# A scheduler's estimate of times in a two-layer hybrid attention kernel: other transfer and operation times, and a port that VectorE and GpSimd share

## The chip, the cores and the metric

The kernel runs on one core of a Trainium2 chip. The metric is device time in microseconds (us) of one execution; lower is better.

## What is computed

The reference takes 1024 tokens of width 1024, puts 16 meta tokens ahead of them, and runs two layers. Each layer normalises, projects to 3588 columns, runs three mixers side by side, gates each with a SiLU, projects back and adds to the residual:

```python
for l in range(DEPTH):                       # 2
    hn = rmsnorm(h, norm_g[l])
    proj = jnp.einsum('bld,de->ble', hn, w_in[l])
    fq, fk, fv, fz, fg, dq, dk, dv, dz, pu, pz = jnp.split(proj, IN_OFFSETS, axis=-1)
    a_out = forgetting_attention(...) * jax.nn.silu(fz)      # 4 heads, causal, with a decay
    ...
    # 4 heads; each is softmax(q0 k0) - lam * softmax(q1 k1), with a distance bias
    b_out = differential_attention(...)
    b_out = rmsnorm(b_out, subln_g[l], SUBLN_EPS) * (1.0 - lambda_init)
    b_out = b_out.reshape(B, Lp, DIFF_W) * jax.nn.silu(dz)
    c_out = pooling_mixer(pu, w_pool[l], pool_scale[l]) * jax.nn.silu(pz)
    mix = jnp.concatenate([a_out, b_out, c_out], axis=-1)
    h = h + jnp.einsum('ble,ed->bld', mix, w_out[l])
y = rmsnorm(h[:, N_META:N_META + S], final_g)
```

All arithmetic is fp32 in effect: each matrix operand is split into two fp32r parts, and TensorE runs three products.

## The kernel before

The normalised input of a layer lies in SBUF (HT). The work of a layer is six "units", one after the other: two with two forgetting heads each, four with one differential head each. A unit projects V, Q and K, and runs its attention as tasks of 256 queries (`jp` 0 to 3). While one unit's attention runs, the projections of the next fill TensorE, and those of the pooling mixer fill it beside the last unit. At the end of the layer the eight mixed blocks go through the output projection.

A differential task makes these instructions. TensorE writes scores into a `psS` bank (three of them). VectorE adds the bias and takes the row minimum (the custom operation `p<-psS,dist` with its reader `mx`), ScalarE takes the exponential, VectorE makes `rd` (a reciprocal), and for the second softmax `n<-rd,nlam` and then `p<-p,n,p`, which combines the two. TensorE transposes `p` into `psT`, ScalarE and VectorE split it into two parts (`pp`), and TensorE multiplies by V into the one `psO` bank; the meta keys go the same way through the copy `m`, a transpose and `ptm`. Then comes the head's normalisation: `sq`, its parts `s` (VectorE a cast, GpSimd the rest), a product with ones, a row `v`, and three small transfers on the queue of SyncE: `rs<-v` turns the row into a column, GpSimd raises it to the power -0.5, `r_d<-rs` writes it to DRAM, and `vr<-r_d` reads it back onto all 128 partitions. VectorE multiplies the task's result by it: `sz<-sz,gs,vr`, which is called the scaling here. There are 32 scalings, 16 in a layer.

GpSimd also subtracts the parts of the weights (`ws<-wr,ws`), of the queries (`q<-rq,q`), and makes the window sums of the pooling mixer (`wa`, `wb`).

Every engine runs its instructions in the order in which they stand in its queue. This order is not the order of the code. `Order` records each instruction with its engine, its operands and an estimated duration (`note`, `cost`), and after the last one `simulate` runs a list schedule over all engines: it takes the instruction that can start first by the estimate (`free`, the end of what its engine runs; `ready`, the end of what it reads, plus `HOP`; `slots`, the time at which a buffer comes free; `way`, the longest way to the end, breaks ties). `tell` fixes the order that comes out, for TensorE, ScalarE, VectorE, GpSimd and the transfers. TensorE's instructions come from six lines (`ordr.line`), each of which keeps its own order; the estimate decides how they are merged. What work stands in which line is set earlier, by the `Clock` and the `Planner`, which the change does not touch.

Of the kernel before, what the change touches and what calls it, by code (L numbers as in the profile page):

```python
# [12 lines left out]
ALU = mybir.AluOpType  # L13
# [36 lines left out]
class Clock:  # L50

    HOP = {"act": 100, "dve": 100, "pool": 150, "dma": 1900}

# [103 lines left out]
class Order:  # L159
# [1 line left out]

    HOP = {"pe": 170, "act": 100, "dve": 100, "pool": 150, "dma": 0}

    def __init__(self):
        self.ops, self.writes, self.reads, self.rings, self.place = [], {}, {}, {}, {}
# [30 lines left out]
                at = [a + s * i for a in at for i in range(n)]  # L198
        return p0, p0 + np_, [(a, a + size) for a in at]

    def add(self, eng, ins, outs, inps, dur, tail=0):
        k, before, names = len(self.ops), set(), set()
        for aps, own, others in ((inps, self.reads, (self.writes,)), (outs, self.writes, (self.writes, self.reads))):
            for ap in aps:
                name = ap.tensor.name
                names.add(name)
                p0, p1, at = self.parts(ap)
                for lo, hi in at:
                    for other in others:
                        old = other.get(name, ())  # L210
                        before.update(e[4] for e in old if e[2] < hi and lo < e[3] and e[0] < p1 and p0 < e[1])
                        if own is self.writes and old:
                            other[name] = [e for e in old if e[0] < p0 or e[1] > p1 or e[2] < lo or e[3] > hi]
                    own.setdefault(name, []).append((p0, p1, lo, hi, k))
        before.discard(k)
        self.ops.append(dict(
            k=k, eng=eng, ins=ins, dur=dur, end=dur + tail + self.HOP[eng], before=sorted(before), stream=self.stream,
            tiles=[n for n in names if n in self.place]))

    def note(self, eng, op, ins, out, inps, extra, kw):  # L220
        dma = "dma" in op
        self.add(eng, ins, [out] + extra, inps, 350 if dma else self.cost(eng, op, out, inps, kw))
        self.ops[-1].update(dma=dma, size=4 * out.free_size() * out.partition_size() if dma else 0)

    @staticmethod
    def cost(eng, op, out, ins, kw):
        n = out.free_size()
        if eng == "act":
            pointers = sum(hasattr(kw.get(k), "tensor") for k in ("bias", "scale"))
            return 150 + 0.88 * n + 95 * pointers + (187 if kw.get("accum_out") is not None else 0)  # L230
        if eng == "dve":
            inner = sum(a.space != bass.MemoryType.PSUM and a.free_size() >= n > 1 for a in ins)
            if op == "memset":
                return 60 + 0.3 * n
            if op == "tensor_tensor_reduce":
                return 230 + 1.05 * n
            if inner == 1 and ins[0].space != bass.MemoryType.PSUM and op in ("tensor_copy", "tensor_scalar"):
                return 190 + 0.6 * n
            return 150 + (1.55 if inner > 1 else 1.05) * n
        if kw.get("op") == ALU.pow:  # L240
            return 400 + 160 * n
        return 180 + {"tensor_tensor": 2.33, "scalar_tensor_tensor": 1.5}.get(op, 3.8) * n

    def prepare(self):
        ops = self.ops
# [30 lines left out]
    def simulate(self):  # L276
        ops = self.ops
        self.prepare()
        left = [len(o["before"]) for o in ops]
        ready = [0.0] * len(ops)  # L280
        start, done = [None] * len(ops), [None] * len(ops)
        engines = ("pe", "act", "dve", "pool", "dma")
# [10 lines left out]
        for o in reversed(ops):  # L293
            if o["eng"] == "pe":
                lines.setdefault(o["stream"], []).append(o["k"])
        pe_prev = (0.0, 0.0)

        def offer(k):
            o = ops[k]
# [24 lines left out]
        while n_done < len(ops):  # L324
            best = None
            for e in engines:
                if e == "pe":
                    c = None
                    for line in lines.values():
                        if not line or left[line[-1]] or (s := slots(line[-1])) is None:  # L330
                            continue
                        load = max(pe_prev[0], pe_prev[1], ready[line[-1]], s)
                        d = (load, 0.0, line[-1], max(free["pe"], load + 105), e)
                        if c is None or d < c:
                            c = d
                    if c is None:
                        continue
                else:
                    c = None
                    for k in waiting[e]:  # L340
                        s = slots(k)
                        if s is None:
                            continue
                        t = max(free[e], ready[k], s)
                        d = (t, -ops[k]["way"], k, t, e)
                        if c is None or d < c:
                            c = d
                    if c is None:
                        continue
                if best is None or c < best:  # L350
                    best = c
            assert best is not None, "no instruction can go on"
            _, _, k, t, e = best
            o = ops[k]
            start[k] = t
            for n in o["tiles"]:
                if self.first[n] == k:
                    tag, i = self.place[n]
                    begun[tag] = i + 1
                    if i >= self.rings[tag][0]:  # L360
                        g = min(gone[tag])
                        gone[tag].remove(g)
                        taken[n] = g[1]
                    else:
                        taken[n] = None
            free[e] = t + o["dur"]
            end = t + o["end"]
            if e == "pe":
                lines[o["stream"]].pop()
                pe_prev = (t, best[0] + 105)  # L370
            else:
                waiting[e].remove(k)
            if e == "dma":
                bus = max(bus, t + 350) + o["size"] / 300.0
                end = max(t + 350 + 1900, bus + 1500)
            done[k] = end
            order[e].append(k)
            n_done += 1
            for n in o["tiles"]:
                uses[n] -= 1  # L380
                lastuse[n] = max(lastuse.get(n, 0.0), end)
                if not uses[n]:
                    gone[self.place[n][0]].append((lastuse[n], n))
            for a in o["after"]:
                left[a] -= 1
                if e != "pe" or ops[a]["eng"] != "pe":
                    ready[a] = max(ready[a], end)
                if not left[a] and ops[a]["eng"] != "pe":
                    offer(a)
# [17 lines left out]
def hymba(  # L407
# [93 lines left out]
    def transpose(o, src, ident):  # L501
        r = nc.tensor.transpose(o, src, ident)  # L502
        clk.pe(o, [src], 0.84 * o.free_size())
        ordr.add("pe", r.ins, [o], [src, ident], 0.447 * o.free_size() + 4.5)

    xs, tail = [], None

# [1028 lines left out]
```

## Time and profile before

| | |
|---|---|
| median of 3 runs | 1269.38 us (1265.15 to 1269.6) |
| the profiled execution, its own time | 1262.05 us |
| its span, from the first to the last instruction | 1260.3 us |

The span and its own time differ by 1.75 us, which lie around the first and the last instruction. In the profile PE is TensorE, DVE is VectorE, ACT is ScalarE, POOL is GpSimd and SP is SyncE; line L148 is the helper through which all operations but those of TensorE are issued, so that groups are told apart by the names of their tiles. A tile's number is left out there. A busy time of PE contains matrix products that overlap, so idle time, and what ended it, tells more than the share.

### The profile page before, as it was taken

What the parts mean: (1) busy time and instruction counts of PE and PEld (TensorE: products, weight loads), DVE (VectorE), ACT (ScalarE), POOL (GpSimd) and SP (SyncE); (2) the same over time, 40 slices, a digit from 0 to 9 for tenths busy, and PEclk for the clock granted to TensorE, in tenths of its full rate; (3) what the DMA queues carried; (4) which work ended last, traced back from release to release, by engine and by line L of the source; (5) the groups of instructions that cost most, each with busy time, mean ns of one, the idle gap of its engine ahead of it and who ended that gap; (6) DMA issues with size and microseconds to landing.
All of it is one profiled execution on the core that took longest, in us unless ns stands there. A gap on an engine that the chain in (4) does not pass through costs nothing.

```text
span 1260.3 us, 21117 instructions
## 1 busy us (share of the span) xinstructions
PE 1202.6 (95%) x7644; PEld 1140.3 (90%) x7644; DVE 831.3 (66%) x2203; ACT 628.8 (50%) x1454; POOL 503.1 (40%) x584
## 2 busy tenths in 40 slices
PE   5999999999998889899999999999999999989997
PEld 4999999999998889878889999999999999989886
DVE  6556868886866848863245568688758687678422
ACT  6555655564554534453235556565545555446222
POOL 6334234345351625464313353241543525254432
PEclk9999999999999989999999999999999999999999
DMA  7121110122222232462110211111212231315431
GB/s 237 26 69 35 51 51 19 51 35 35 55 35 46 50 89 49 111 207 97 67 51 24 63 35 60 43 26 43 35 40 54 38 59 31 95 33 158 142 111 50
DMA packets 101736, 82.12 MB, mean 65 GB/s; under 512 B 19272, under 2 KB 91208, under 8 KB 101632
## 3 DMA queue, kind: packets, MB, share of 16 engines
q1 hardware_dynamic: 101488, 80.52, 24.3%
q8 instruction: 60, 0.98, 0.3%
q14 instruction: 44, 0.36, 0.1%
q10 hardware_dynamic: 144, 0.26, 0.1%
HBM read 66.92 MB, written 13.80 MB: 64 GB/s over the span
## 4 chain that ended last, share of the span: by engine, by line
PE 72%; DVE 10%; DMA 9%; POOL 3%; issue 3%; ACT 1%; SPq 0%; POOLq 0%; DVEq 0%; ACTq 0%
PE psP L496 47%; PE psS L496 13%; PE psT L502 6%; PE psO L496 6%; DMA vr<-r_d 4%; DVE p L148 4%; DMA r_d<-rs 3%; POOL q L148 1%; DVE sz L148 1%; DVE q L148 1%; POOL rs L148 1%; PE psS L502 1%; DMA x<-in_x_dram 1%; DVE pp L148 1%; DVE n L148 1%
## 5 line engine op out<-in xcount | busy, mean ns | idle before, releaser
L496 PE MATMUL psP<-HT,ws 128*128 128x346 f32 (+5 forms) x4032 | 714.8, 326 | 3.2 <-DVE Y L148 2.2
L496 PEld LDWEIGHTS psP<-HT,ws 128*128 128x128 f32 x4032 | 644.3, 190 | 5.4 <-DVE Y L148 2.6
L148 POOL TENSOR_TENSOR ws<-wr,ws 128x512 fp32r<-128x512 f32 x112 | 152.6, 1364 | 229.4 <-ACT ws L148 171.8
L148 POOL TENSOR_TENSOR q<-rq,q 64x256 fp32r<-64x256 f32 (+1 forms) x192 | 149.8, 780 | 128.8 <-DVE q L148 94.9
L148 ACT ACTIVATE p<-p,mx 128x144 f32<-128x144 f32 (+3 forms) x192 | 150.8, 786 | 76.8 <-DVE mx L148 74.2
L496 PE MATMUL psS<-K,q 128*128 128x392 f32 (+9 forms) x696 | 145.9, 330 | 9.4 <-DVE mx L148 9.4
L496 PE MATMUL psO<-pp,VV 128*128 128x256 f32 (+1 forms) x800 | 123.4, 284 | 2.1 <-DVE pp L148 2.1
L496 PEld LDWEIGHTS psS<-K,q 128*128 128x128 f32 (+1 forms) x696 | 108.6, 189 | 12.5 <-DVE mx L148 10.9
L496 PE MATMUL psP<-HT,ms 128*128 128x512 f32 (+1 forms) x504 | 115.4, 385 | 2.3 <-ACT HT L148 1.6
L148 DVE TENSOR_TENSOR pp<-psT,pp 128x512 fp32r<-128x512 f32 (+1 forms) x160 | 98.3, 632 | 23.6 <-ACT pp L148 22.0
L496 PEld LDWEIGHTS psO<-pp,VV 128*128 128x128 f32 x800 | 111.4, 191 | 2.7 <-DVE pp L148 2.6
L148 ACT ACTIVATE pp<-psT 128x512 fp32r<-128x512 f32 (+1 forms) x160 | 84.6, 551 | 58.2 <-PE psT L502 53.7
L496 PEld LDWEIGHTS psP<-HT,ms 128*128 128x128 f32 x504 | 90.6, 188 | 22.8 <-ACT HT L148 2.1
L502 PE MATMUL psT<-identf,p 128*128 128x128 f32 x576 | 88.9, 274 | 7.4 <-DVE p L148 6.7
L148 ACT ACTIVATE ws<-wr 128x512 fp32r<-128x512 f32 x112 | 70.3, 629 | 49.4 <-PE psP L496 24.5
L502 PEld LDWEIGHTS psT<-identf,p 128*128 128x128 f32 x576 | 69.0, 141 | 11.3 <-DVE p L148 8.8
L148 DVE TENSOR_SCALAR p<-p,rd 128x144 f32<-128x144 f32 (+7 forms) x128 | 77.2, 604 | 1.5
L148 DVE CUSTOM_DVE_ANT_0 p<-psS,dist 128x272 f32<-128x272 f32 (+7 forms) x128 | 62.1, 492 | 21.6 <-PE psS L496 15.8
L496 PE MATMUL psS<-HT,ms 128*128 128x512 f32 (+2 forms) x320 | 75.4, 394 | 0.0
L496 PEld LDWEIGHTS psS<-HT,ms 128*128 128x128 f32 (+2 forms) x320 | 57.6, 180 | 16.7
L148 ACT ACTIVATE K<-psP 64x346 fp32r<-64x346 f32 (+1 forms) x72 | 32.6, 453 | 74.4 <-DVE K L148 50.2
L148 POOL TENSOR_TENSOR ms<-mr,ms 128x128 fp32r<-128x128 f32 (+2 forms) x39 | 33.4, 862 | 81.9 <-ACT ms L148 81.8
(132 smaller groups left out, 1452.7 us busy)
## 6 DMA issues: line engine op xcount, KB each, us to landing
wr<-in_w_in_dram SPq DMA_DIRECT2D x112, 256.0 KB
wo<-in_w_out_dram SPq DMA_DIRECT2D x14, 512.0 KB
mr<-mix_d SPq DMA_DIRECT2D x14, 320.0 KB
cb<-c_d SPq DMA_DIRECT2D x8, 520.0 KB
x<-in_x_dram SPq DMA_DIRECT2D x8, 512.0 KB
res<-in_x_dram SPq DMA_DIRECT2D x8, 512.0 KB
h_d<-res SPq DMA_DIRECT2D x8, 512.0 KB
res<-h_d SPq DMA_DIRECT2D x8, 512.0 KB
```

Of the source, the lines that this page charges most:

```text
L148: r = f(*args, **kw)
L496: r = nc.tensor.matmul(o, w, m, start=start, stop=stop)
L502: r = nc.tensor.transpose(o, src, ident)
```

## The change

The estimate is changed in five ways, and nothing else is.

- `HOP`, the time from the end of an instruction to the start of one that waits for it, falls from 100 or 150 to 38 ns for ScalarE, VectorE and GpSimd, and rises from 170 to 200 ns for TensorE.
- A transfer was taken to land the later of 2250 ns after its issue and 1500 ns after its bytes had passed a bus of 300 bytes/ns. It now lands 1900 ns after its issue, plus its bytes at 330 bytes/ns (with the transfers queued on one bus), plus 1600 ns if it reads one row onto all partitions, or 1100 ns if its rows are shorter than 8 elements.
- VectorE's and GpSimd's operations have a flag, `port`: true for all of GpSimd's, and for those of VectorE that read SBUF alone (some copies and reductions excepted). An operation with the flag does not start before the last flagged one of the other engine has ended.
- The formulas of `cost` have other numbers; the two-input operations of VectorE in SBUF, which were taken 1.55 ns per element, are now 1.04 ns.
- TensorE's separate model of the weight load is gone; a transpose is 109 ns and no longer 62.

```diff
-    HOP = {"pe": 170, "act": 100, "dve": 100, "pool": 150, "dma": 0}
+    HOP = {"pe": 200, "act": 38, "dve": 38, "pool": 38, "dma": 0}
...
     def note(self, eng, op, ins, out, inps, extra, kw):
-        dma = "dma" in op
-        self.add(eng, ins, [out] + extra, inps, 350 if dma else self.cost(eng, op, out, inps, kw))
-        self.ops[-1].update(dma=dma, size=4 * out.free_size() * out.partition_size() if dma else 0)
+        if "dma" in op:
+            size = 4 * out.free_size() * out.partition_size()
+            more = 1600 if inps[0].ap[0][0] == 0 else 1100 if out.ap[-1][1] < 8 else 0
+            self.add("dma", ins, [out], inps, 350)
+            self.ops[-1].update(size=size, extra=more, end=2000 + more + size / 330.0)
+            return
+        dur, port = self.cost(eng, op, out, inps, extra, kw)
+        self.add(eng, ins, [out] + extra, inps, dur, port)
 
     @staticmethod
-    def cost(eng, op, out, ins, kw):
+    def cost(eng, op, out, ins, extra, kw):
+
         n = out.free_size()
+        sbuf = all(a.space != bass.MemoryType.PSUM for a in ins)
+        pointers = sum(hasattr(kw.get(k), "tensor") for k in ("bias", "scale", "scalar"))
         if eng == "act":
-            pointers = sum(hasattr(kw.get(k), "tensor") for k in ("bias", "scale"))
-            return 150 + 0.88 * n + 95 * pointers + (187 if kw.get("accum_out") is not None else 0)
-        if eng == "dve":
-            inner = sum(a.space != bass.MemoryType.PSUM and a.free_size() >= n > 1 for a in ins)
-            if op == "memset":
-                return 60 + 0.3 * n
-            if op == "tensor_tensor_reduce":
-                return 230 + 1.05 * n
-            if inner == 1 and ins[0].space != bass.MemoryType.PSUM and op in ("tensor_copy", "tensor_scalar"):
-                return 190 + 0.6 * n
-            return 150 + (1.55 if inner > 1 else 1.05) * n
-        if kw.get("op") == ALU.pow:
-            return 400 + 160 * n
-        return 180 + {"tensor_tensor": 2.33, "scalar_tensor_tensor": 1.5}.get(op, 3.8) * n
+            return 165 + 35 * sbuf + 0.835 * n + 80 * pointers + 95 * len(extra), False
+        if eng == "pool":
+            if kw.get("op") == ALU.pow:
+                return 400 + 160 * n, True
+            return 180 + {"tensor_tensor": 2.33, "scalar_tensor_tensor": 1.5}.get(op, 3.8) * n, True
+        if op == "memset":
+            return 60 + 0.3 * n, False
+        if op == "tensor_tensor_reduce":
+            return 158 + 1.05 * n + 63 * pointers, False
+        if op == "reciprocal":
+            return 157, False
+        if not sbuf or op == "tensor_tensor_scan":
+            return 150 + 1.05 * n, False
+        if op == "tensor_copy" or op == "tensor_scalar":
+            if len(ins[0].ap) > len(out.ap) or any(d[0] == 0 for d in ins[0].ap):
+                return 146 + 1.04 * n, False
+            return (146 if op == "tensor_copy" else 213) + 0.523 * n, True
+        return (150 if op == "tensor_tensor" else 220) + 1.04 * n, True
...
-        pe_prev = (0.0, 0.0)
+        port = dict.fromkeys(engines, 0.0)
...
-                        load = max(pe_prev[0], pe_prev[1], ready[line[-1]], s)
-                        d = (load, 0.0, line[-1], max(free["pe"], load + 105), e)
+                        t = max(free["pe"], ready[line[-1]] + 20, s + 20)
+                        d = (t, 0.0, line[-1], t, e)
...
+                        if ops[k]["port"]:
+                            t = max(t, port["dve" if e == "pool" else "pool"])
...
+            if o["port"]:
+                port[e] = free[e]
...
-                bus = max(bus, t + 350) + o["size"] / 300.0
-                end = max(t + 350 + 1900, bus + 1500)
+                bus = max(bus, t + 900) + o["size"] / 330.0
+                end = bus + 1000 + o["extra"]
...
-        ordr.add("pe", r.ins, [o], [src, ident], 0.447 * o.free_size() + 4.5)
+        ordr.add("pe", r.ins, [o], [src, ident], max(109, 0.447 * o.free_size() + 4.5))
```

The orders that come out hold the same instructions. Three places show how they differ. The names in the rows carry tile numbers; ISA is the custom operation with its reader.

The first is TensorE's queue in a differential unit of layer 0, at the scores of its second task (`jp` 1). `psT_5034` and `psT_5041` take the transposes of the first task, `psS_5056` and `psS_5060` are the two halves of a row of scores, and each needs a free `psS` bank. Before:

```order
753 L496 MATMUL psP_4928<-HT,ws_4664 128x346 x6
754 L496 MATMUL psP_5021<-HT,ws_4659 128x346 x12
755 L502 MATMUL psT_5034<-identf,p_4908 128x128
756 L496 MATMUL psS_5056<-K_1029_4655,q_4628 128x264 x2
757 L496 MATMUL psS_5060<-K_1029_4655,q_4628 128x264 x2
758 L496 MATMUL psP_5021<-HT,ws_4664 128x346 x3
759 L502 MATMUL psT_5034<-identf,p_4950 128x128 x2
```

And with the change:

```order
753 L511 MATMUL psP_5021<-HT,ws_4659 128x346 x12
754 L517 MATMUL psT_5034<-identf,p_4908 128x128
755 L517 MATMUL psT_5034<-identf,p_4950 128x128 x2
756 L517 MATMUL psT_5041<-identf,m_1120_5042 96x16
757 L517 MATMUL psT_5041<-identf,m_1121_5045 96x128
758 L517 MATMUL psT_5041<-identf,m_1122_5048 96x128
759 L511 MATMUL psS_5056<-K_1029_4655,q_4628 128x264 x2
760 L511 MATMUL psS_5060<-K_1029_4655,q_4628 128x264 x2
761 L511 MATMUL psP_5021<-HT,ws_4664 128x346 x12
```

The transposes of the first task now stand ahead of the scores. In VectorE's queue at the same place the scaling (`sz_3873<-sz_3873,gs_3913,vr_4935`) stood ahead of `rd_4975`, and now stands 18 instructions later, behind the bias operations of these scores and the split of the transposes. The next unit has the same two differences.

The second place is VectorE's queue in the third differential unit of layer 1, with the scaling of `vr_13186`. Before:

```order
1966 L148 COPY m_2867_13274<-p_13159 128x96
1967 L148 SCALAR_TENSOR_TENSOR sz_12155<-sz_12155,gs_12195,vr_13186 128x256
1968 L148 ISA p_13218,mx_13219<-psS_13220,dist 128x400
1969 L148 ISA mx_13219 128x1
1970 L148 ISA p_13248,mx_13249<-psS_13250,dist 128x264
1971 L148 ISA mx_13249 128x1
1972 L148 TENSOR_TENSOR pp_13267<-psT_13263,pp_13267 128x384
```

And with the change:

```order
1969 L148 COPY m_2867_13274<-p_13159 128x96
1970 L148 ISA p_13218,mx_13219<-psS_13220,dist 128x400
1971 L148 ISA mx_13219 128x1
1972 L148 ISA p_13248,mx_13249<-psS_13250,dist 128x264
1973 L148 ISA mx_13249 128x1
1974 L148 TENSOR_TENSOR pp_13267<-psT_13263,pp_13267 128x384
1975 L148 SCALAR_TENSOR_TENSOR sz_13092<-th_13243,psP_13179 128x346
1976 L148 TENSOR_TENSOR ptm_13277<-psT_13270,ptm_13277 32x256
1977 L148 SCALAR_TENSOR_TENSOR sz_12155<-sz_12155,gs_12195,vr_13186 128x256
1978 L148 ISA p_13248,mx_13249<-psS_13254,dist,mx_13249 128x264
```

The scaling let seven instructions pass, and none of the other rows shown moved. Of the 32 scalings 26 are passed by 1 to 32 instructions in this way, and six by none; one of the six is the scaling of `vr_10775`, the first of layer 1.

The third place is TensorE's queue in the second differential unit of layer 1, at the transposes of the last task (`jp` 3). `p_11815` is the output of `p<-p,n,p`. Before:

```order
1799 L496 MATMUL psP_11984<-HT,ws_11716 128x348 x6
1800 L502 MATMUL psT_12003<-identf,p_11726 128x128
1801 L496 MATMUL psP_11984<-HT,ws_11716 128x348 x6
1802 L502 MATMUL psT_12003<-identf,p_11815 128x128
1803 L502 MATMUL psT_12003<-identf,p_11726 128x128
```

And with the change:

```order
1804 L511 MATMUL psP_11984<-HT,ws_11716 128x348 x6
1805 L517 MATMUL psT_12003<-identf,p_11726 128x128
1806 L517 MATMUL psT_12003<-identf,p_11815 128x128
1807 L517 MATMUL psT_12003<-identf,p_11726 128x128
1808 L517 MATMUL psT_12003<-identf,p_11815 128x128
```

Six matrix products no longer stand between the first transpose and the one that needs `p_11815`. On VectorE the scaling and one cast of queries, which stood ahead of `p_11815<-p_11889`, now stand behind it.

## Rows read from the trace of the kernel before

**Rows 1.** The page's first part: span, then busy time, share, instructions of TensorE.

```profile
span 1260.3 us, 21117 instructions
PE 1202.6 (95%) x7644; PEld 1140.3 (90%) x7644; DVE 831.3 (66%) x2203; ACT 628.8 (50%) x1454; POOL 503.1 (40%) x584
```

**Rows 2.** Windows: stretch, length, busy time of each engine, granted clock, DMA share, GB/s.

```profile
core 0: us, PE busy (x) PEld busy (x) DVE busy (x) ACT busy (x) POOL busy (x), PEclk, DMA share, GB/s
31.50:283.50 252.00, 250.54 (x1734) 246.04 (x1733) 179.07 (x540) 144.04 (x337) 92.11 (x100) 1.00 0.16 42
283.50:535.50 252.00, 234.65 (x1532) 227.90 (x1531) 182.84 (x518) 122.76 (x287) 107.31 (x108) 0.97 0.27 59
661.50:882.00 220.50, 219.98 (x1526) 217.03 (x1525) 152.74 (x439) 126.05 (x289) 78.77 (x87) 1.00 0.15 42
882.00:1134.00 252.00, 237.41 (x1557) 232.59 (x1556) 184.98 (x501) 128.07 (x289) 109.13 (x114) 0.97 0.25 48
```

**Rows 3.** VectorE's largest wait: total, times, longest us.

```profile
DVE sz L148 <- DMA vr<-r_d: 56.1, 18, 6.7
```

**Rows 4.** Timeline of one transfer chain, layer 0: start, us, engine, instruction, idle before.

```profile
454.96 0.48 SPq L148 DMA_DIRECT2D rs<-v  x1
...
457.14 0.69 POOL L148 TENSOR_TENSOR rs<-rs,nhalf 128x2 f32<-128x2 f32 x1 [1.33 <-DMA rs<-v]
...
457.86 0.34 SPq L148 DMA_DIRECT2D r_d<-rs  x1
...
460.70 0.34 SPq L148 DMA_DIRECT2D vr<-r_d  x1
...
464.55 0.48 DVE L148 SCALAR_TENSOR_TENSOR sz<-sz,gs,vr 128x256 f32<-128x256 f32 x1 [4.78 <-DMA vr<-r_d]
...
465.18 0.57 DVE L148 CUSTOM_DVE_ANT_0 p<-psS,dist 128x400 f32<-128x400 f32 x1
...
465.82 0.81 PE L496 MATMUL psS<-K,q 128*128 128x264 f32 x2 [3.58 <-DVE mx L148]
```

**Rows 5.** Timeline, TensorE alone: other waits behind a scaling that waited.

```profile
304.53 0.71 PE L496 MATMUL psP<-HT,ws 128*128 128x346 f32 x3 [1.00 <-DVE K L148]
...
387.21 0.81 PE L496 MATMUL psS<-K,q 128*128 128x264 f32 x2 [3.25 <-DVE mx L148]
...
528.39 0.90 PE L496 MATMUL psP<-HT,ws 128*128 128x348 f32 x4 [2.20 <-DVE Y L148]
...
897.67 0.50 PE L496 MATMUL psO<-pp,VV 128*128 128x256 f32 x2 [2.07 <-DVE pp L148]
...
927.79 0.39 PE L496 MATMUL psT<-s,onesr 128*128 128x256 f32 x1 [1.55 <-DVE s L148]
...
1086.29 1.11 PE L496 MATMUL psS<-K,q 128*128 128x264 f32 x4 [2.14 <-DVE mx L148]
...
1113.50 0.39 PE L496 MATMUL psO<-ptm,VM 96*128 96x256 f32 x1 [3.48 <-DVE ptm L148]
```

**Rows 6.** Three like products at either clock, and a window behind a wait.

```profile
141.65 0.69 PE L496 MATMUL psP<-HT,ws 128*128 128x348 f32 x3
...
387.81 1.07 PE L496 MATMUL psP<-HT,ws 128*128 128x346 f32 x3
...
383.00:390.40 7.40, 4.15 (x19) 3.48 (x18) 3.68 (x14) 1.73 (x4) 1.27 (x1) 0.77 0.38 89
```

**Rows 7.** VectorE beside GpSimd: a tile's operation (ns min/median/max), then timeline.

```profile
L148 DVE TENSOR_TENSOR n<-rd,nlam x68: 136/159/3070, 231.5 to 1149.4; 128x1 f32<-128x1 f32 x64, 16x1 f32<-16x1 f32 x4
...
430.64 1.40 DVE L148 SCALAR_TENSOR_TENSOR sz<-sz,gs,vr 128x256 f32<-128x256 f32 x1 [0.54 <-DMA vr<-r_d]
...
435.13 0.55 PE L502 MATMUL psT<-identf,p 128*128 128x128 f32 x3 [2.20 <-DVE p L148]
...
1052.14 3.07 DVE L148 TENSOR_TENSOR n<-rd,nlam 128x1 f32<-128x1 f32 x1
1052.67 2.51 POOL L148 TENSOR_TENSOR ws<-wr,ws 128x512 fp32r<-128x512 f32 x2
...
1056.87 0.33 PE L502 MATMUL psT<-identf,p 128*128 128x128 f32 x1 [2.27 <-DVE p L148]
```

More of the change, by code (lines that the diff above doesn't have):

```diff
@@ L199, in parts, with add @@
         return p0, p0 + np_, [(a, a + size) for a in at]
-    def add(self, eng, ins, outs, inps, dur, tail=0):
+    def add(self, eng, ins, outs, inps, dur, port=False):
         k, before, names = len(self.ops), set(), set()
@@ L216, in add @@
         self.ops.append(dict(
-            k=k, eng=eng, ins=ins, dur=dur, end=dur + tail + self.HOP[eng], before=sorted(before), stream=self.stream,
+            k=k, eng=eng, ins=ins, dur=dur, port=port, end=dur + self.HOP[eng], before=sorted(before), stream=self.stream,
             tiles=[n for n in names if n in self.place]))
     def note(self, eng, op, ins, out, inps, extra, kw):
-        dma = "dma" in op
-        self.add(eng, ins, [out] + extra, inps, 350 if dma else self.cost(eng, op, out, inps, kw))
@@ L367, in simulate @@
             end = t + o["end"]
+            if o["port"]:
+                port[e] = free[e]
             if e == "pe":
                 lines[o["stream"]].pop()
-                pe_prev = (t, best[0] + 105)
             else:
```

## Prediction

> **What bounds the kernel now.** I read the page first, then windows, the waits of VectorE, and timelines around TensorE's waits. TensorE is busy for 1202.6 of 1260.3 us [rows 1], so an order can win no more than its 57.7 us of idle time and what a lowered clock costs. The windows show where that idle time lies. The stretches 31.5 to 283.5 and 661.5 to 882 us hold 1.46 and 0.52 us of it; 283.5 to 535.5 and 882 to 1134 us hold 17.35 and 14.59 us, and there the granted clock is 0.97 [rows 2]. These two hold most of the differential heads of the two layers, and most of the scalings.
>
> VectorE's largest wait says why: it stands idle 56.1 us in 18 waits before scalings, for the transfer `vr<-r_d` [rows 3]. One chain shows it in full [rows 4]. The three transfers were issued at 454.96, 457.86 and 460.70 us, and the scaling began at 464.55 us. From one issue to the next step the first took 2.18 us, the second 2.84 and the third 3.85; with GpSimd's step the whole took 9.59 us. The estimate of before gives each transfer some 2.25 us, so it ends about 2 us too early, and the scaling stands that much too early in VectorE's queue. Behind it stood the bias operation that frees a `psS` bank (465.18 us), and TensorE waited 3.58 us for that bank. So the reader is to see that the wait for a transfer costs nothing by itself; what stands behind it in the queue does.
>
> **The change part by part.**
>
> *Transfers.* By the new formulas `rs<-v` and `r_d<-rs` take 3.0 us each and `vr<-r_d` 3.9 us: 0.8 us over the first duration read above, 0.2 over the second, and equal to the third within 0.1. The scalings therefore move behind the work that TensorE waits for. I went through TensorE's waits that follow a waiting scaling and asked of each whether the instruction waited for now stands ahead of the scaling:
>
> - 3.58 us [rows 4] and, at 387.21, 3.25 us [rows 5]: these are the first place shown and its twin in the next unit; 18 instructions pass the scaling, and the transposes stand ahead of the scores. Both go.
> - 1.00 us at 304.53: the two `K` operations pass it. 2.20 us at 528.39: the operation that writes `Y` passes it. 1.55 us at 927.79: the cast of `s` passes it. 2.14 us at 1086.29: the second place shown. 3.48 us at 1113.50: `ptm` passes it [rows 5].
> - 2.07 us at 897.67 stays: the scaling of `vr_10775` is passed by none.
>
> The six waits to be removed, and the seventh in the timeline of the chain, sum to 3.58 + 3.25 + 1.00 + 2.20 + 1.55 + 2.14 + 3.48 = 17.2 us. The scalings themselves have no reader soon, apart from the last of a layer, so that their delay is hidden by the next unit's attention; the last scaling of layer 0 does not move and that of layer 1 moves by one instruction. Where a scaling moves less far than its transfer is late, a stall stays. At 1086.29 seven instructions pass, five of them operations; at the 0.57 us of such a row [rows 4] that is at most 2.9 us, and the transfer may be later than that. For such remainders I give back 1.7 us.
>
> *The clock.* Behind the two longest waits the granted clock falls to the lower of its two levels, 1.2 instead of 2.4 GHz: 0.77 over 383.0 to 390.4 us, and three like products take 1.07 us instead of 0.69 [rows 6]. That is 0.38 us at least. At most it is half of the 3.4 us which a mean of 0.77 implies at the lower level, 1.7 us. TensorE was also idle in a part of these 3.4 us, so I take 1.0 us for each of the two places: 2.0 us.
>
> *The port.* `n<-rd,nlam`, an operation on one column, takes 159 ns in the middle and 3070 ns once, when GpSimd ran two weight subtractions beside it [rows 7]. The two engines shut each other out. TensorE waited 2.20 us at 435.13 and 2.27 us at 1056.87 for a `p` that was late this way. At the first the scaling itself took 1.40 us ahead of `p`; the new order takes it out from there, which I count at 1.9 us of the 2.20, the scaling with the 0.54 us that it waited. At the second, the scaling moves behind `p`, but `n` still meets GpSimd: I count 0.5 us, about the time of an undisturbed scaling [rows 4]. Together 2.4 us; bounds are 0 and 4.47 us.
>
> The Trainium skill, SBUF — State Buffer, section "Who interferes with whom", says that the pair of ports is an exclusive lock, and that the second instruction blocks until the first has finished. The trace agrees that there is a lock, but the 3.07 us are longer than one GpSimd instruction beside it. By the rule the port term would be 4.47 us, by the row 2.4.
>
> *What it can cost.* The new order trusts its estimate and takes cover away. At the third place shown, six matrix products no longer stand between the first transpose and the one that needs `p_11815`; six take 1.07 x 2 = 2.1 us at the lower clock and 0.69 x 2 = 1.4 us at the higher [rows 6]. `p` is earlier there, since the scaling and a cast no longer stand ahead of it. But where a weight subtraction comes in its way, it is late by one: two took 2.51 us, so one is 1.26 us [rows 7]. I give back one, 1.3 us; the bounds are nothing and the rival below.
>
> *Hop, durations, weight load.* They move instructions by a few tenths of a microsecond at many places, under the projections that fill TensorE in the two quiet stretches (1.98 us idle in 472.5 us [rows 2]). The old figures already left almost nothing there, so I count zero, and 2 us either way. The start and the two output projections I count at nothing as well, for their products stand in the same order but for a few transposes.
>
> **The sum.** 17.2 + 2.0 + 2.4 - 1.7 - 1.3 = 18.6 us. The profiled execution took 1262.05 us, 1.75 around its span [rows 1]: 1243.5 us. The median of the runs shown is 1269.38, 0.58% above that execution; by the same ratio the forecast is 1250.7, say **1251 us**. Its own range is 1243 to 1260.
>
> **The rivals.**
>
> - *The lock is kept exactly.* If an operation that is shut out always gets in after one instruction, as the new estimate has it, both port waits go and nothing is given back: 17.2 + 2.0 + 4.5 = 23.7 us. At the far end all idle time of the two stretches but that of the quiet ones goes, 31.9 - 2.1 + 2.0 = 31.8 us. In the profile that is 1230 to 1238 us, 1237.5 to 1245.5 us on the median. This is what the rule of the Trainium skill, SBUF — State Buffer, "Who interferes with whom", makes of it. For it: most of the `n` are near 159 ns. Against it: the 3070.
> - *The stalls move.* The scalings leave, but TensorE then waits for the next thing in the same chains, `p` from ScalarE and VectorE, so that 0 to 4 us remain of the gain: 1265 to 1270 us. For it: VectorE is busy 182.84 and 184.98 us of 252 in the two stretches [rows 2], so little slack is left where work is pressed together. Against it: it stood idle for 56.1 us for transfers alone.
> - *Slower: the cover is missed.* Each of the 32 differential tasks ends with `p<-p,n,p` and its transposes. If GpSimd's subtractions fall beside `p` in most of them, each costs 1.26 us with no product left to cover it. It takes more than 18.6 + 1.3 = 19.9 us, so 16 of the 32, to be slower than before; in 30 of them it is 1262.05 - 19.9 + 37.8 = 1280 us, 1287 on the median. For it: 2.51 us of two subtractions in a row. Against it: only the two waits in the rows look like this before, and the new estimate knows of the lock.
>
> **How the numbers follow.** The forecast has 0.60, the exact lock 0.16, the moved stalls 0.16, the slower case 0.08. A change under 0.5% (6 us) can't be told from none by this measurement. The forecast and the exact lock are faster by more than that, and so is a small part of the moved stalls: 0.78. The rest of the moved stalls is no change, 0.14; slower is 0.08. The range from 1238 to 1267 us takes in the forecast, nearly all of the exact lock and half of the moved stalls; it leaves out the slower case and some 0.1 more.
>
> **What would show it.** After the change VectorE's wait for `vr<-r_d` should fall from 56.1 to under 20 us, and TensorE's idle time in the stretches of the differential heads from 31.9 to some 14 us, with fewer falls of the granted clock. The places named should hold no wait of TensorE over 1 us, apart from the one behind `vr_10775`. The forecast is wrong if the wait for `vr<-r_d` falls and the idle time of TensorE does not, with waits for `p` or `pp` in its place; or if `n<-rd,nlam` and `p<-p,n,p` grow and TensorE waits behind them in most tasks.

## The result, and the profile after

The changed kernel takes 1239.1 us (median of 4 runs, 1238.0 to 1240.6), against 1269.5 us before (4 runs, 1265.2 to 1271.2): a ratio of 0.9767, with a 95% interval of 0.974 to 0.9793. In a second measurement it was 0.9781 (0.9747 to 0.9815). It is faster, by more than the forecast of 1251 us; the time lies inside the whole range and below the forecast's own.

The page's first part, after (answers to [rows 1]):

```profile
span 1238.8 us, 21122 instructions
PE 1199.4 (97%) x7644; PEld 1136.7 (92%) x7644; DVE 805.1 (65%) x2203; ACT 628.4 (51%) x1454; POOL 499.1 (40%) x584
```

The span is 21.5 us shorter. TensorE's idle time, span less busy time, falls from 57.7 to 39.4 us, which is 18.3 of it; its busy time falls by 3.2 us with the same 7644 instructions, which fits the fewer falls of the granted clock in the windows below. VectorE's 2203 instructions take 26.2 us less, though none was removed.

Windows of the same stretches (answer to [rows 2]; the columns are those there):

```profile
31.50:283.50 252.00, 251.16 (x1733) 245.85 (x1732) 175.42 (x537) 144.00 (x335) 90.71 (x101) 1.00 0.16 41
283.50:535.50 252.00, 244.14 (x1618) 238.44 (x1618) 183.36 (x536) 132.35 (x310) 116.09 (x118) 0.99 0.32 65
661.50:882.00 220.50, 219.66 (x1518) 215.43 (x1517) 158.35 (x454) 127.55 (x293) 81.49 (x90) 1.00 0.17 45
882.00:1134.00 252.00, 244.24 (x1624) 241.29 (x1624) 184.86 (x518) 131.36 (x295) 111.29 (x116) 0.98 0.31 59
```

The two stretches of the differential heads now hold 7.86 and 7.76 us of idle time, together 15.6, where they held 31.9. Their granted clock rose from 0.97 to 0.99 and 0.98. The quiet stretches hold 1.7 us (2.0 before).

VectorE's wait for the transfer (answers to [rows 3]: total, times, longest us):

```profile
DVE sz L148 <- DMA vr<-r_d: 9.1, 5, 5.5
```

Timeline at the place of [rows 4], after:

```profile
445.04 0.48 SPq L148 DMA_DIRECT2D rs<-v  x1
...
447.83 0.69 POOL L148 TENSOR_TENSOR rs<-rs,nhalf 128x2 f32<-128x2 f32 x1 [1.76 <-DMA rs<-v]
...
448.55 0.34 SPq L148 DMA_DIRECT2D r_d<-rs  x1
...
451.19 0.34 SPq L148 DMA_DIRECT2D vr<-r_d  x1
...
456.20 0.42 DVE L148 CUSTOM_DVE_ANT_0 p<-psS,dist 128x264 f32<-128x264 f32 x1
...
457.60 0.48 DVE L148 CUSTOM_DVE_ANT_0 p<-psS,dist,mx 128x264 f32<-128x264 f32 x1
...
458.08 0.47 DVE L148 SCALAR_TENSOR_TENSOR sz<-sz,gs,vr 128x256 f32<-128x256 f32 x1
458.11 0.66 PE L511 MATMUL psS<-K,q 128*128 128x264 f32 x4
```

The transfers are no faster: over the 32 `vr<-r_d` of this kernel the time from issue to landing is 3.8 us at least, 4.3 in the middle and 6.9 at most:

```profile
DMA to landing us min/median/max: 3.8/4.3/6.9
```

So the new 3.9 us is still under the middle one, and 9.1 us of wait are left. At the place shown the scaling now begins 6.89 us after the last issue (it was 3.85), waits for nothing, and stands behind the bias operations that free the `psS` bank; the scores go on without the 3.58 us.

TensorE's own waits, after (total, times, longest us), show what is left:

```profile
PE psS L517 <- DMA identf<-in_ident_dram: 10.1, 1, 10.1
PE psP L511 <- DVE Y L148: 6.6, 2, 3.6
PE psT L517 <- DVE p L148: 4.1, 7, 0.8
PE psS L517 <- DVE wg L148: 2.9, 1, 2.9
PE psP L511 <- ACT pu L148: 2.9, 1, 2.9
```

The waits for `mx` have shrunk away and none for `p` is over 0.8 us. Besides the start, where the first and the `wg` row lie, the three waits over 1 us are those for `Y` and `pu`, in the pooling mixer at the end of each layer; together they are 9.5 us.

### The profile page after: what moved, and what is told of

Read it like the earlier page. It is cut to its first block, busy times and chain, and to the rows that moved or that the text cites. A ratio compares the mean times of both kernels' runs of the same rounds, so it can differ in the third digit from the quotient of the medians.

```text
span 1238.8 us, 21122 instructions
## 1 busy us (share of the span) xinstructions
PE 1199.4 (97%) x7644; PEld 1136.7 (92%) x7644; DVE 805.1 (65%) x2203; ACT 628.4 (51%) x1454; POOL 499.1 (40%) x584
## 3 DMA queue, kind: packets, MB, share of 16 engines
q1 hardware_dynamic: 101488, 80.52, 26.2%
## 4 chain that ended last, share of the span: by engine, by line
PE 85%; DVE 7%; ACT 3%; DMA 2%; issue 2%; SPq 0%; POOL 0%; POOLq 0%; ACTq 0%; DVEq 0%
PE psP L511 56%; PE psS L511 14%; PE psO L511 7%; PE psT L517 7%; DVE p L148 3%; DMA wo<-in_w_out_dram 1%; ACT p L148 1%; PE psS L517 1%; DVE pp L148 1%; DMA x<-in_x_dram 1%; PE psT L511 1%; DVE HT L148 0%; SPq L148 0%; DMA m<-in_m_dram 0%; DVE Y L148 0%
## 5 line engine op out<-in xcount | busy, mean ns | idle before, releaser
L148 DVE TENSOR_SCALAR p<-p,rd 128x144 f32<-128x144 f32 (+7 forms) x128 | 74.0, 582 | 1.7
L148 DVE CUSTOM_DVE_ANT_0 p<-psS,dist 128x272 f32<-128x272 f32 (+7 forms) x128 | 61.9, 490 | 12.8 <-PE psS L511 7.0
```

The lines of the kernel that those rows point to most:

```text
L148: r = f(*args, **kw)
```

## The experiments

The first runs take the change apart into transfers (the new landing times), port (the exclusion) and numbers (`HOP`, `cost`, TensorE's model). They fill all eight combinations, so each part can be read in four pairs. The kernel before ran at a median of 1259 us on the chip of `a`, `b`, `c` and `d` and at 1266 to 1269 us in the other measurements, so kernels of different chips are compared by their ratios. The changed kernel was not run on the chip of `a` to `d`; that a ratio carries over from chip to chip is assumed, not shown.

| kernel | transfers | port | numbers | ratio to before | 95% interval | TensorE idle, us | VectorE busy, us | wait for `vr<-r_d`, us |
|---|---|---|---|---|---|---|---|---|
| before | old | no | old | 1 | | 57.7 | 831.3 | 56.1 |
| a_transfers_only | new | no | old | 0.9847 | 0.9823 to 0.9871 | 46.0 | 833.8 | 9.4 |
| d_port_only | old | yes | old | 0.9912 | 0.9889 to 0.9935 | 47.5 | 797.4 | 31.0 |
| e_numbers_only | old | no | new | 1.0245 | 1.0205 to 1.0285 | 79.9 | 833.5 | 66.3 |
| f_transfers_port | new | yes | old | 0.9823 | 0.9791 to 0.9856 | 45.3 | 788.5 | 13.4 |
| c_no_port | new | no | new | 0.9895 | 0.9872 to 0.9918 | 47.3 | 835.8 | 12.8 |
| b_old_transfers | old | yes | new | 1.0063 | 1.0042 to 1.0083 | 58.7 | 804.4 | 28.2 |
| after | new | yes | new | 0.9767, 0.9781 | 0.974 to 0.9815 | 39.4 | 805.1 | 9.1 |

The last three columns come from the profiled execution of each; idle is span less busy time.

**Transfers alone.** `a_transfers_only`, the kernel before with:

```diff
+            more = 1600 if inps[0].ap[0][0] == 0 else 1100 if out.ap[-1][1] < 8 else 0
+            self.ops[-1].update(size=size, extra=more, end=2000 + more + size / 330.0)
...
-                bus = max(bus, t + 350) + o["size"] / 300.0
-                end = max(t + 350 + 1900, bus + 1500)
+                bus = max(bus, t + 900) + o["size"] / 330.0
+                end = bus + 1000 + o["extra"]
```

> The kernel before, with the new times of the transfers alone; hop, operation times and TensorE's model stay old, and there is no port. Theory (the scalings stood too early, and the transfer times put them right): this part carries most of the gain. By the sum of the prediction it is 17.2 + 2.0 - 1.7 = 17.5 us, and up to 25 us if the waits at the port go as well because the scaling has left; so a ratio to before of 0.980 to 0.987, VectorE's wait for vr<-r_d from 56.1 to under 20 us, and the waits for p behind a shut-out n or p stay. Rival one (the port carries it): 0.992 to 1.0, with the wait for vr<-r_d down and TensorE's idle time not. Rival two (hop and operation times carry it): 0.990 to 1.0.

Measured: 0.9847, 19 us, inside the theory's range. The wait for `vr<-r_d` is 9.4 us, and the waits behind the lock are still there. TensorE's timeline, at the two places of the port term [rows 7]:

```profile
430.58 0.66 PE L506 MATMUL psT<-identf,p 128*128 128x128 f32 x4 [1.53 <-DVE p L148]
...
1036.46 1.52 PE L506 MATMUL psT<-identf,p 128*128 128x128 f32 x7 [2.08 <-DVE p L148]
```

**Transfers undone.** `b_old_transfers` is the changed kernel with the lines with a minus above in place of those with a plus.

> The changed kernel with the transfer times of before; port, hop and operation times stay new. Theory: most of the gain is lost, since the scalings stand too early again; against before 0.990 to 1.0, the wait for vr<-r_d back over 40 us, and waits of TensorE over 1 us behind waiting scalings in both differential stretches. Rival one (port): 0.977 to 0.985. Rival two (hop and operation times): 0.978 to 0.988.

Measured: 1.0063, slower than before. Without the transfers the rest of the change is worse than nothing; rivals one and two fall. The theory had the side right, but its range ended at 1.0, and it had the wait for `vr<-r_d` back over 40 us, where 28.2 were measured: the port holds a part of it down (see `d_port_only`).

**Port undone, and port alone.** `c_no_port` leaves two lines out of the changed kernel; `d_port_only` puts the port into the kernel before:

```diff
-                        if ops[k]["port"]:
-                            t = max(t, port["dve" if e == "pool" else "pool"])
```

> The changed kernel without the port: VectorE's and GpSimd's operations no longer wait for each other in the estimate; all else as in the changed kernel. Theory: 1 to 5 us above the changed kernel, so 0.977 to 0.982 against before, with some n<-rd,nlam of 2 to 3 us back. Rival one (the port carries the gain): 0.985 to 1.0, more than 10 us above the changed kernel. Rival two: no difference from the changed kernel within 2 us.

> The kernel before with the port alone; all times as before. Theory: 0.995 to 1.0 against before, the longest n<-rd,nlam below 1.5 us where it was 3070 ns, the wait for vr<-r_d still over 40 us. Rival one (the port carries the gain): 0.978 to 0.988. Rival two: 1.0.

Measured: 0.9895 and 0.9912. Both miss the theory to the same side: the port is worth 0.9% by itself (11 us), and 1.1 to 1.3% beside the rest, where I expected 5 or 6 us at most. `c_no_port` even lies in the range of rival one, that the port carries the gain; only `b_old_transfers` rules it out as the sole carrier. The other two pairs give 0.2% beside the new transfers alone (`a_transfers_only` to `f_transfers_port`, intervals overlapping) and 1.8% beside the new numbers alone (`e_numbers_only` to `b_old_transfers`): the port is worth more with the new numbers than with the old. The long `n<-rd,nlam` were no sign of it: the theory had some of 2 to 3 us back in `c_no_port`, but the longest there is 1.27 us, as in `a_transfers_only`, which has no port either (1.26). The pages show a part of where it works. VectorE's busy time of `d_port_only`, then of `c_no_port`:

```profile
PE 1196.6 (96%) x7644; PEld 1134.1 (91%) x7644; DVE 797.4 (64%) x2203; ACT 627.3 (50%) x1454; POOL 500.0 (40%) x584
```

```profile
PE 1197.9 (96%) x7644; PEld 1133.4 (91%) x7644; DVE 835.8 (67%) x2203; ACT 627.2 (50%) x1454; POOL 504.7 (41%) x584
```

An operation that is shut out counts as busy: in [rows 7] `n` on one column was busy for 3.07 us. The same 2203 instructions take 831 to 836 us in the four kernels of the table without the port, and 789 to 805 in the four with it; in the four pairs that differ by the port alone it takes 29 to 45 us out of VectorE's queue. How much of that reaches TensorE differs: its idle time falls by 0.7 us (beside the transfers) to 21.2 us (beside the numbers). By itself the port also brings the wait for `vr<-r_d` from 56.1 to 31.0 us, where the theory had over 40, though it says nothing of transfers. So a part of its 11 us can be stalls that the new landing times remove as well; how much was not separated.

**The changed kernel again, and numbers alone.** `e_numbers_only` is the changed kernel with the edits of `b_old_transfers` and `c_no_port` together.

> The changed kernel itself, beside the others on one chip. In both theories 0.974 to 0.980 against before, as in its first measurement.

> The changed kernel with the transfer times of before and without the port, so that only hop, operation times and TensorE's model are new. The runs so far give two estimates of what these numbers are worth: beside the new transfers they cost 7.1 us (1247.4 less 1240.2), beside the port 19.9 us (1268.6 less 1248.7). First theory (they tighten the order and are harmful while the transfers are estimated too short): 1.005 to 1.016 against before, with VectorE's wait for vr<-r_d over 40 us. Second theory (the effects of order are chance): anything from 0.985 to 1.015, without a larger wait for vr<-r_d. The prediction's own count was zero, 2 us either way: 0.998 to 1.002.

Measured: 0.9781 and 1.0245. The numbers alone cost 31 us (0.0245 of 1268.2), more than the first theory said, and with its mark: the wait for `vr<-r_d` is up to 66.3 us in 22 waits, the most of all. Its timeline shows one of them:

```profile
386.78 0.34 SPq L148 DMA_DIRECT2D vr<-r_d  x1
...
391.47 0.48 DVE L148 SCALAR_TENSOR_TENSOR sz<-sz,gs,vr 128x256 f32<-128x256 f32 x1 [5.10 <-DMA vr<-r_d]
391.87 0.49 DVE L148 SCALAR_TENSOR_TENSOR p<-p,n,p 128x272 f32<-128x272 f32 x1
...
392.42 0.69 PE L514 MATMUL psT<-identf,p 128*128 128x128 f32 x2 [4.42 <-DVE p L148]
```

The scaling stands ahead of the `p` that TensorE needs, and 4.42 us go.

**Transfers and port, old numbers.** `f_transfers_port` is the kernel before with the edits of `a_transfers_only` and `d_port_only`.

> The kernel before with the new transfer times and the port; hop, operation times and TensorE's model old. If the parts add up: 18.9 and 10.4 us, 0.977 against before. First theory (the two parts make the gain, the numbers nothing): 0.974 to 0.982, within 4 us of the changed kernel. Rival (the lock can only be planned for with the new operation times, so they belong to the gain): 0.983 to 0.990, over 8 us above the changed kernel.

Measured: 0.9823 (1243.9 us), 4.7 us above the changed kernel beside it (1239.2), just outside the first theory, which had at most 0.982 and 4 us. So transfers and port carry 1.8 of the 2.2% on this chip. The numbers, harmful by themselves, seem to give the last 0.4%, though the two intervals overlap.

**Is it chance?** `g_hop60` shifts the estimate a little; `l_late_vr` makes `vr<-r_d` wrong to the other side:

```diff
-    HOP = {"pe": 200, "act": 38, "dve": 38, "pool": 38, "dma": 0}
+    HOP = {"pe": 200, "act": 60, "dve": 60, "pool": 60, "dma": 0}
```

```diff
-            more = 1600 if inps[0].ap[0][0] == 0 else 1100 if out.ap[-1][1] < 8 else 0
+            more = 4600 if inps[0].ap[0][0] == 0 else 1100 if out.ap[-1][1] < 8 else 0
```

> The changed kernel with 60 instead of 38 ns for the hop of ScalarE, VectorE and GpSimd; 22 ns are less than any wait spoken of, but some 970 of 4300 lines of VectorE's order differ. First theory (the gain is made by the scalings' and the lock's places): within 4 us of the changed kernel. Second theory (any shift of the estimate deals the stalls anew): over 8 us away from it, to either side, with stalls of TensorE over 1 us at other places.

> The changed kernel with the estimate of a transfer that reads one row onto all partitions (vr<-r_d) 3.0 us longer than the new one: wrong by as much as the old one, to the other side. Theory (a scaling that stands too late costs nothing, since it has no reader soon; only too early costs): within 5 us of the changed kernel, 0.974 to 0.982 against before, VectorE's wait for vr<-r_d at most the 9.1 us of the changed kernel. Rival (the estimate must be right to either side): over 8 us above the changed kernel.

Measured: 0.9777 (0.9738 to 0.9817), 0.5 us from the changed kernel, and 0.9791 (0.9765 to 0.9816). One other order with the same time and the same list of TensorE's waits speaks against chance as the source of the whole gain; it does not say that parts of 5 us, such as those of the next runs, are free of it. Exactness doesn't explain the gain either. With `vr<-r_d` estimated 3 us too long, VectorE has no wait for it at all, and the time is that of the changed kernel within its interval: what matters for this transfer is that its estimate isn't too short.

**What is left.** The waits for `Y` lead to a transfer of 512 bytes. In the changed kernel (a tile's instructions, ns min/median/max, first and last start):

```profile
L148 SPq DMA_DIRECT2D sc<-in_pool_scale_dram x4: 422/422/423, 494.6 to 1101.7; - x4
...
  PE psP L511: 6.6, 2
```

`Y<-psP,sc` can't go before `sc` (the second row: TensorE waits 6.6 us behind its readers). `sc` depends on nothing, but shares a ring of 24 buffers with all one-column tiles, and so is issued only at the end of its layer. The trace does not show `Y` waiting for it, though: the scale landed 2.7 us after its issue, some 6 us before `Y<-psP,sc` began, which stood behind the reader of the window sums in VectorE's queue. Rows of the changed kernel, then of `i_own_scale`:

```profile
494.58 0.90 SPq L148 DMA_DIRECT2D sc<-in_pool_scale_dram  x2
...
501.52 1.28 DVE L148 SCALAR_TENSOR_TENSOR Y<-wb,invw,Y 128x1024 f32<-128x1024 f32 x1
...
503.88 1.07 DVE L148 TENSOR_SCALAR Y<-psP,sc 128x348 f32<-128x348 f32 x2
```

```profile
500.04 1.07 DVE L148 TENSOR_SCALAR Y<-psP,sc 128x348 f32<-128x348 f32 x2 [0.52 <-PE psP L511]
...
502.65 1.28 DVE L148 SCALAR_TENSOR_TENSOR Y<-wb,invw,Y 128x1024 f32<-128x1024 f32 x1
```

So the late load works through the estimate, which gives `Y` its place. `i_own_scale` gives it a ring of its own, `k_win_only` corrects the estimate of GpSimd's window sums, `j_own_scale_win` does both:

```diff
-            sc = keep["sc"] = sm("sc")
+            sc = keep["sc"] = small.tile([128, 1], F32, tag="sc", name=nm("sc"), bufs=4)
...
-            return 180 + {"tensor_tensor": 2.33, "scalar_tensor_tensor": 1.5}.get(op, 3.8) * n, True
+            return ((100 + 1.75 * n) if op == "tensor_tensor" and n > 600 else 180 + {"tensor_tensor": 2.33, "scalar_tensor_tensor": 1.5}.get(op, 3.8) * n), True
```

> The changed kernel, with the load of pool_scale (sc) in four buffers of its own instead of the 24 that all one-column tiles share. In the changed kernel sc is issued at 1101.23 us of the span, 2.7 us before it lands, and Y<-psP,sc, for which TensorE waits 3.02 us in layer 0 and 3.57 us in layer 1, can't go before it. Theory (what is left at the layers' ends is this late load): both waits shrink below 2 us, and the time falls by 3 to 7 us against the changed kernel, 0.972 to 0.976 against before. Rival (Y is late through VectorE's queue and the window sums): within 2 us of the changed kernel, Y<-psP,sc still late.

> As the run before, and the estimate of GpSimd's long two-input operations (over 600 columns) is 100 + 1.75 ns a column instead of 180 + 2.33, since the window sums of 1038 columns took 1.92 us in the changed kernel and 2.60 us are counted. Theory (the chain of the window sums is counted too long, so its readers stand too late): another 3 to 7 us, 0.966 to 0.973 against before, with no wait of TensorE over 2.5 us after the start. Rival (any shift deals the stalls anew): between 3 us faster and 5 us slower than the run before.

> The changed kernel with the shorter estimate of GpSimd's window sums alone; the load of pool_scale stays in the shared buffers. With both it was 0.9681 against before, with the own buffers alone 0.9768, and the changed kernel 0.9767 and 0.9781. First theory (Y needs both its window sums and its scale in time, so that either alone leaves the other as the last to come): 0.973 to 0.978, waits of TensorE for Y over 2 us still there. Second theory (the window sums are the whole of it): 0.967 to 0.971.

Measured: 0.9768 (0.9742 to 0.9795), 0.9681 (0.9658 to 0.9705) and 0.9822 (0.9798 to 0.9847). Neither alone gains anything clear of noise; together they are the best kernel of the study, 1227.2 us, 10.7 us under `i_own_scale` beside it, where the theory had 3 to 7. In `i_own_scale` `sc` is issued by 21.6 us and the waits for `Y` are gone, as the theory said, but the time is that of its rival: the two differential stretches hold 4.4 us less idle time, and the output projection of layer 0 gives back 2.4 of it. That it gives them back in `j_own_scale_win` too (3.7 us idle there) says that this is not what parts the two. Its window, in the changed kernel and then in `i_own_scale`:

```profile
535.50:661.50 126.00, 124.64 (x610) 100.56 (x610) 47.45 (x74) 41.90 (x105) 45.49 (x72) 1.00 0.30 95
```

```profile
535.50:661.50 126.00, 122.28 (x591) 98.22 (x590) 46.56 (x75) 41.43 (x104) 44.39 (x70) 0.99 0.27 89
```

With the sums corrected as well, layer 1's stretch is full to 0.55 us and no wait for `Y` or `pu` is among TensorE's largest. Windows of `j_own_scale_win`, then its waits of TensorE:

```profile
283.50:535.50 252.00, 245.88 (x1639) 239.23 (x1638) 186.64 (x544) 137.12 (x325) 119.12 (x121) 1.00 0.34 72
882.00:1134.00 252.00, 251.45 (x1704) 248.96 (x1704) 190.45 (x532) 141.26 (x319) 119.77 (x124) 1.00 0.34 67
```

```profile
PE psS L517 <- DMA identf<-in_ident_dram: 9.8, 1, 9.8
PE psT L517 <- DVE p L148: 4.1, 7, 0.8
PE psS L517 <- DVE wg L148: 3.1, 1, 3.1
```

In `k_win_only` the late `sc` holds VectorE itself once, and a `p` is 5.82 us late, but before that; rows of its two timelines:

```profile
1117.92 1.06 DVE L148 TENSOR_SCALAR Y<-psP,sc 128x348 f32<-128x348 f32 x2 [1.80 <-DMA sc<-in_pool_scale_dram]
```

```profile
1115.88 1.76 PE L517 MATMUL psT<-identf,p 128*128 128x128 f32 x7 [5.82 <-DVE p L148]
```

No theory had named this: one wait for `Y` over 2 us remains (2.34), but the shorter estimate with `sc` still late is some 5 us dearer than the changed kernel's second measurement (the intervals overlap). The wait for `sc` comes after the late `p` and so did not make it late. From 1107.87 us to the end of this `p` VectorE worked through its queue with waits of 0.15 and 0.48 us; what put `p` at the end of that is not settled.

## Why the prediction came out as it did

The direction and the main cause were right, the size was too small: 1251 against 1239.1 us. The miss of 11.9 us has two parts.

- *The sum* was 18.6 us; the profiled executions differ by 21.4 (1262.05 to 1240.62). Its terms without the clock, 16.6 us, stand against 18.3 us of idle time, and the clock's 2.0 us against 3.2 us of busy time. So 2.8 us of the miss are the sum's, by these two executions.
- *The step to the median* failed. I kept the ratio of median to profiled execution, 1.0058, but the changed kernel's median is 1.5 us below its profiled execution. That is the other 9 us. One execution was a poor base: in the second measurement the kernel before took 1260.7 us in one of seven runs, at a granted clock of 0.992, and 1269.8 at 0.987 in another. The profiled execution lay below all four runs of its kernel shown in the result, and the ratio carried that over to a kernel whose own profiled execution is the longest of its four. Set median against median, the gain is 30.4 us and the sum 11.8 short of it; what the other executions before lose beyond the profiled one was not traced.

That the sum came so near in the profiled executions is in part luck. Going by the ratios from the kernel before over `a_transfers_only` and `c_no_port` to the changed kernel, the transfers gave 1.5%, the numbers took 0.5% and the port gave 1.1 to 1.3%, where the sum had 1.4% (17.5 us), nothing, and 0.2% (2.4 us). A port that was counted too small and numbers that were counted as harmless partly cancel.

Point by point:

- **Transfers, 17.2 - 1.7 us and the clock: right.** Six of the seven waits are gone. The seventh, for `Y`, no longer stands behind a scaling, but one for `Y` is back 24 us earlier (3.02 us at 504.52), from the other cause found above. `a_transfers_only` measures 19 us where this part says 17.5. The three new durations were not all right: 3.9 us for `vr<-r_d` is below the 4.3 us of the middle landing. `vr<-r_d` fell to 9.1 us (said: under 20), idle time in the two stretches to 15.6 us (said: some 14). That it is the scaling's place in the queue is shown by `l_late_vr` and `e_numbers_only`.
- **The wait behind `vr_10775` was said to stay, and went.** Its scaling still waits 1.14 us, but TensorE has no wait over 1 us there. I looked only at what passes the scaling, not at what else moved ahead of TensorE's need.
- **The port, 2.4 us, bounds 0 and 4.47: mis-sized.** In the place that it has in the sum, beside all the rest, it is 1.1 to 1.3%, 14 to 16 us (8 us if the medians of the two chips are set side by side), and alone 11 us; beside the new transfers with the old numbers it would have been about right, 0.2% or 3 us. I read the lock's price from the two waits of TensorE behind it; it was spread over VectorE's queue, as 29 us and more of busy time, and what of it reaches TensorE hangs on the other parts. At the two places themselves 1.60 and 1.72 us went (2.20 and 2.27 became 0.60 and 0.55), 3.3 in all.
- **The lock miss where cover was taken, 1.3 us: not seen.** No wait for `p` is over 0.8 us.
- **Hop, durations, weight load at zero, 2 us either way: failed as a step.** Alone they cost 31 us, beside the transfers 0.5%, beside the port 1.5%, beside both the best reading is a gain of 0.4%. The parts don't add up, and a term of zero for one of them was a statement about the other two.
- **The rivals.** The time falls into the band of the exact lock, but not by its mechanism: the lock is not kept (last section). The stalls moved in part: the waits for `Y` and `pu`, 4.1 us before (2.20 of it in [rows 5]), are 9.5 after. The slower case did not come.

Why the new numbers alone make so many scalings early was not tested. That the shorter operations let VectorE run ahead in the estimate, so that a scaling fills a hole that isn't there, is argued only.

## What to carry to other kernels

In a list schedule over queues that run in order, the error to fear is a wait estimated too short: whatever stands behind the waiting instruction pays, while an estimate 3 us too long cost nothing for a scaling, which has no reader soon. Where there are readers, too long can cost as well: the window sums were counted 0.7 us too long, and correcting that was worth 10.7 us once the scale's load was early. Correct the estimates together: sharper operation times on top of short transfers cost 31 us, a shorter window sum on top of a late load seems to cost 5 us. And a load without inputs can still be late through the ring that it shares; look at its issue before the arithmetic behind it.

## What the runs showed of the hardware

- A shut-out operation can still wait for more than one instruction of the other engine, though the estimate lets it wait for one. In the changed kernel `p<-p,n,p` on 1040 columns took 3.06 us once, beside three of GpSimd's, and 1.30 us in `k_win_only` with GpSimd idle. After the first of the three alone, which ended at 425.06 us, it would have ended at 426.36 us; it ended at 427.41. GpSimd's two subtractions were held too, 3.51 us for what takes 1.29 each. The rule of the Trainium skill that the prediction weighed (SBUF — State Buffer, "Who interferes with whom": blocked until the first has finished) does not cover this. VectorE's row, then the one of `k_win_only`, then GpSimd's of the changed kernel:

```profile
424.35 3.06 DVE L148 SCALAR_TENSOR_TENSOR p<-p,n,p 128x1040 f32<-128x1040 f32 x1
```

```profile
1114.52 1.30 DVE L148 SCALAR_TENSOR_TENSOR p<-p,n,p 128x1040 f32<-128x1040 f32 x1
```

```profile
424.33 0.73 POOL L148 TENSOR_TENSOR q<-rq,q 64x256 fp32r<-64x256 f32 x1 [0.23 <-DVE n L148]
425.03 3.51 POOL L148 TENSOR_TENSOR ws<-wr,ws 128x512 fp32r<-128x512 f32 x2
```

- GpSimd's time per column falls with the length. Instructions of two tiles of the changed kernel:

```profile
L148 POOL TENSOR_TENSOR wb<-wa x6: 1917/1922/2437, 478.0 to 1098.9; 128x1038 f32<-128x1038 f32 x2, 64x1032 f32<-64x1032 f32 x2, 64x1038 f32<-64x1038 f32 x2
```

```profile
L148 POOL TENSOR_TENSOR ws<-wr,ws x112: 1264/1292/2268, 18.6 to 1122.8; 128x512 fp32r<-128x512 f32 x112
```

  512 columns take 1.29 us and 1038 take 1.92: 1.2 ns for each further column, not the 2.33 of the estimate. The short one writes another type, so that length may not be all of it.
- From the issue of `vr<-r_d` to its scaling 4.69 us passed in `e_numbers_only`, against 3.85 in [rows 4], and the landings of the changed kernel reach from 3.8 to 6.9 us; a landing time read at one place is no bound.
